# Fixed orders in a Fourier layer without GpSimd, a padded Nyquist product, and seven block products in another order

## The chip, the cores and the metric

One core of a Trainium2 chip runs the whole program. The metric is the device time of that core in microseconds for one execution, as the median of the runs. Its engines are called PE (TensorE's matmuls; PEld is its weight loads), DVE (VectorE), ACT (ScalarE), POOL (GpSimd) and SP (SyncE, which starts the DMAs here).

## What is computed

Two trunk layers over 512 tokens of 1024 channels, with a context of 256 tokens. Layer 0 has attention, layer 1 Fourier mixing; both end with a gated ConvFFN. All data is float32. Cut to the parts that the change touches:

```python
D_MODEL, SEQ, FNET_GROUPS, D_FF = 1024, 512, 4, 2816

def fourier_mix(h):                                   # layer 1
    hg = h.reshape(b, l, FNET_GROUPS, d // FNET_GROUPS).astype(F32)
    f = jnp.fft.fft2(hg, axes=(1, 3), norm="ortho").real
    return f.reshape(b, l, d).astype(h.dtype)

def conv_ffn(h, w_up, conv_w, conv_b, w_down):        # both layers
    u = h @ w_up
    up = jnp.pad(u, ((0, 0), (1, 1), (0, 0)))
    u = up[:, :-2] * conv_w[0] + up[:, 1:-1] * conv_w[1] + up[:, 2:] * conv_w[2] + conv_b
    gate, val = jnp.split(u, 2, axis=-1)
    return (jax.nn.silu(gate) * val) @ w_down
...
    h = modulate(rms_norm(x, norm_g[i, 0]), sh1, sc1)
    y = attention_mixers(...) if i % 2 == 0 else fourier_mix(h) @ w_f
    x = x + g1 * rms_norm(y, norm_g[i, 1])
    h = modulate(rms_norm(x, norm_g[i, 2]), sh2, sc2)
    x = x + g2 * rms_norm(conv_ffn(h, ffn_w_up[i], ffn_conv_w[i], ffn_conv_b[i], ffn_w_down[i]), norm_g[i, 3])
```

## The kernel before

**Numbers.** Every float32 operand of a matmul is kept as a high part (rounded to TensorE's fp32r) and a low part (the rest). `mm3` (L107) makes a product of three matmuls: high by high (L108), high by low (L109), low by high (L110), each up to 128 rows deep and some 256 columns wide. `split` (L130) makes such a pair: ScalarE casts the high part, VectorE subtracts it for the low part (L131). Weights come by DMA into one of three `raw` buffers and are split into `wh` and `wl`.

**Layout.** Channels lie on the 128 partitions in `KC = 8` chunks, the 512 tokens on the free dimension in two halves of 256 (`halves`). `xT` is the residual stream, `yT` the output of a sub-layer before its norm, `hh`/`hl` the pair of the normed input. A `misc` or `mm` tile is one PSUM bank of 512 columns.

**What sets the order.** The code is written in one order, and a scheduler then orders each engine's queue by priorities and dependencies. `follow(i, j)` puts one instruction behind another on the same engine; `fence` and `held` keep what comes after a fence behind what came ahead of it; `behind_pe` starts a generator's TensorE work behind the last matmul so far; `later(n)` lowers or raises the priority.

**Blocks of the FFN.** Layer 0 takes 10 and layer 1 takes 14 of its chunks of up-projection by a seven-product scheme: `seven_products` (L1329) makes two output tiles `x` and `y`, each one PSUM bank of two halves, from seven products "1" to "7" of 12 matmuls each. Products 1, 5, 6 and 7 are needed in two places: ScalarE copies them from PSUM to `xs` or `ys` (L1349, L1351, L1354, L1359), the next product on that bank is added on top or goes to its other half, and VectorE adds the copies to `x` and `y` (L1357, L1360). In code order the products are 1, 5, 2, 6, 4, 3, 7; only the first on a bank and those behind it are tied by `follow`. Around them run VectorE's sums of weights (L1315 to L1318), its low weights and the convolution (L1412 to L1426).

**The Fourier stage.** Between layer 0's last down products (`part(d, [1])`, second half of the tokens, d = 1 to 7) and the output panels of layer 1 the kernel ends layer 0's norm, updates `x`, and transforms. `Plain.tiles` (L410) does it for a half: the statistics' row is spread over the partitions (L234), `x_update` multiplies `yT` by the factor `der` and the row `Rs` and adds it to `xT` (L330, L332), ScalarE makes `hh` (L417), VectorE `hl` (L418), ScalarE the square (L421), and GpSimd sums six of eight chunks' squares (L423). `columns` (L478) turns those sums into a column by matmuls against ones (L483): r, the inverse norm of every token of the next input, which scales rows of the transform. `over_channels(g, h)` transforms a group's 256 channels for a half of the tokens (12 matmuls, and from them `Z`), `group(g, ts)` transforms over the token tiles `ts` of 128, six matmuls for each (cosines into A, sines into B), `tables` makes the token tables `ct` and `st`, the second half's scaled by r. `shift` transforms the constant shift. Channel 128 of each group, the Nyquist channel, has a product of its own: `cosines(None, N, ...)` gives `N`, four rows (one for each group) of 258 columns.

**Output panels.** For each of the eight panels d of 128 output channels: four products of B (12 matmuls) into `pq`, one of N (three matmuls, four rows deep, with the weights `nyh`, `nyl`) and four of A (12 matmuls) into `pp`; ScalarE copies `pq` to `qs` (L1814) and VectorE adds and subtracts the two.

## Time and profile before

| | |
|---|---|
| median of 3 runs | 1110.64 us (1109.5 to 1110.91) |
| the profiled execution | 1112.16 us |
| its span, first to last instruction | 1110.4 us |
| mean granted TensorE clock | 0.996 |
| matmuls recorded | 9220 |
| time that PE and DVE are busy | 97% and 81% of the span |

The profile is of one execution. Its page gives each engine's busy time; the trace behind it gives each instruction's start and length, and for an engine that stood idle what ended the wait, in brackets: `[1.12 <-POOL yT L423]` is 1.12 us idle, ended by GpSimd's write of `yT` on line 423. Rows of tiles read output<-inputs, then partitions x elements. Stages, by the trace: attention until about 320, layer 0's ConvFFN until about 665, the Fourier layer from there to about 729 (its output panels from 700.6), layer 1's ConvFFN until about 1085, then the end.

### The profile page before, as it was taken

The page shows a single profiled execution, that of the slowest core. Times are in us where ns is not written, and L with a number is a line of the kernel's source. Part 1 is how long each engine was busy: PE and PEld are TensorE (multiplying, and loading weights), DVE is VectorE, ACT ScalarE, POOL GpSimd, SP SyncE. Part 2 cuts the span into 40 slices and gives each one's busy share as a digit, 9 for nine tenths or more (in the row PEclk, how much of TensorE's full clock was granted, in tenths as well). Part 3 has the DMA queues.
Part 4 walks back from the last instruction along what each step waited for, and adds up shares of the span by engine and source line. Part 5 has one row for each costly group of instructions (what it writes and reads, how often), then busy time and mean ns, then how long its engine had stood idle before and what let it go on. Part 6 is the DMA issues. An engine that isn't in the chain of part 4 may idle for free.

```text
span 1110.4 us, 22277 instructions
## 1 busy us (share of the span) xinstructions
PE 1081.1 (97%) x9220; PEld 1011.4 (91%) x9220; DVE 894.8 (81%) x1459; ACT 595.2 (54%) x1048; POOL 128.5 (12%) x136
## 2 busy tenths in 40 slices
PE   9999999999999999999999998999999999999995
PEld 5699888869999999999999997989999999999995
DVE  5778877763689967878999788878997998979756
ACT  4442356665665633552556446668755654655543
POOL 0046123412100000000000133300000000000012
PEclk9999999999999999999999999999999999999998
DMA  9675100273231565227624600923205433332342
GB/s 368 273 256 209 39 7 33 76 275 143 77 153 43 181 233 213 106 86 272 236 77 175 231 22 21 279 82 143 86 29 198 145 107 118 105 103 88 106 148 77
DMA packets 33774, 156.01 MB, mean 140 GB/s; under 512 B 3460, under 2 KB 8196, under 8 KB 22024
## 3 DMA queue, kind: packets, MB, share of 16 engines
q1 hardware_dynamic: 32520, 150.39, 37.6%
q0 software_dynamic: 1152, 4.19, 1.5%
q8 instruction: 72, 1.18, 0.4%
q14 instruction: 30, 0.25, 0.1%
HBM read 148.28 MB, written 6.29 MB: 139 GB/s over the span
## 4 chain that ended last, share of the span: by engine, by line
PE 69%; DVE 18%; ACT 6%; DMA 4%; issue 2%; POOL 1%; SPq 0%; DVEq 0%; POOLq 0%; ACTq 0%
PE mm L108 20%; PE mm L109 18%; PE mm L110 18%; DVE wl L131 4%; ACT wh L131 2%; PE PT L1081 1%; DVE cv L1413 1%; DVE cv L1415 1%; DMA raw<-in_w_up 1%; DVE md_t L330 1%; DVE xT L332 1%; PE gm L108 1%; ACT yT L352 1%; PE O L109 1%; PE gm L110 1%
## 5 line engine op out<-in xcount | busy, mean ns | idle before, releaser
L131 ACT CAST wh<-raw 128x1024 fp32r<-128x1024 f32 (+2 forms) x207 | 190.7, 932 | 147.3 <-PE mm L109 96.9
L131 DVE TENSOR_TENSOR wl<-raw,wh 128x1024 fp32r<-128x1024 f32 (+2 forms) x205 | 219.4, 1076 | 59.3 <-ACT wh L131 56.7
L108 PE MATMUL mm<-hh,wh 128*128 128x256 f32 x856 | 240.2, 282 | 2.5 <-ACT sq L1351 1.8
L110 PE MATMUL mm<-hh,wl 128*128 128x256 f32 x856 | 236.9, 277 | 1.7 <-DVE wl L131 1.7
L109 PE MATMUL mm<-hl,wh 128*128 128x256 f32 x856 | 237.0, 277 | 0.4 <-DVE hl L355 0.3
L108 PEld LDWEIGHTS mm<-hh,wh 128*128 128x128 f32 x856 | 160.4, 188 | 8.5 <-ACT sq L1351 6.1
L110 PEld LDWEIGHTS mm<-hh,wl 128*128 128x128 f32 x856 | 160.9, 188 | 2.2 <-DVE wl L131 2.1
L109 PEld LDWEIGHTS mm<-hl,wh 128*128 128x128 f32 x856 | 160.8, 188 | 0.8 <-DVE hl L355 0.5
L108 PE MATMUL mm<-xh,wh 128*128 128x256 f32 x492 | 136.8, 279 | 0.0
L109 PE MATMUL mm<-xl,wh 128*128 128x256 f32 x492 | 136.6, 278 | 0.0
L110 PE MATMUL mm<-xh,wl 128*128 128x256 f32 x492 | 136.4, 277 | 0.0
L108 PE MATMUL mm<-zh,wh 128*128 128x256 f32 x384 | 109.4, 285 | 0.7 <-ACT sq L1354 0.5
L109 PE MATMUL mm<-zl,wh 128*128 128x256 f32 x384 | 106.3, 277 | 0.0
L110 PE MATMUL mm<-zh,wl 128*128 128x256 f32 x384 | 106.2, 277 | 0.0
L108 PEld LDWEIGHTS mm<-xh,wh 128*128 128x128 f32 x492 | 92.4, 188 | 1.2 <-issue 0.8
L109 PEld LDWEIGHTS mm<-xl,wh 128*128 128x128 f32 x492 | 92.4, 188 | 0.6 <-issue 0.4
L110 PEld LDWEIGHTS mm<-xh,wl 128*128 128x128 f32 x492 | 92.5, 188 | 0.1
L108 PEld LDWEIGHTS mm<-zh,wh 128*128 128x128 f32 x384 | 72.1, 188 | 6.0 <-ACT sq L1354 5.4
L110 PEld LDWEIGHTS mm<-zh,wl 128*128 128x128 f32 x384 | 72.2, 188 | 0.0
L109 PEld LDWEIGHTS mm<-zl,wh 128*128 128x128 f32 x384 | 72.1, 188 | 0.0
L305 POOL TENSOR_TENSOR gacc<-gacc,sq 128x256 f32<-128x256 f32 (+1 forms) x23 | 20.2, 880 | 396.8 <-ACT sq L303 396.4
L1412 ACT ACTIVATE cv<-mm,cols 128x512 f32<-128x512 f32 x59 | 45.8, 778 | 10.8 <-PE mm L110 6.1
(457 smaller groups left out, 2795.7 us busy)
## 6 DMA issues: line engine op xcount, KB each, us to landing
raw<-in_w_up SPq DMA_DIRECT2D x42, 1024.0 KB, 4.9
xT<-in_mod_r SPq DMA_DIRECT2D x20, 1024.0 KB, 5.0
raw<-in_w_down SPq DMA_DIRECT2D x32, 384.0 KB, 3.1
raw<-in_mod_p SPq DMA_DIRECT2D x8, 1024.0 KB, 5.0
raw<-in_w_down SPq DMA_DIRECT2D x16, 512.0 KB, 4.3
raw<-in_w_in SPq DMA_DIRECT2D x6, 1024.0 KB, 8.2
yT<-in_mod_r SPq DMA_DIRECT2D x10, 512.0 KB, 6.6
raw<-in_w_out SPq DMA_DIRECT2D x4, 1024.0 KB, 5.9
```

The source lines that it names most:

```text
L108: i = PE.matmul(out, lhsT=ah, rhs=bh, start=start, stop=False, skip_group_check=skip)
L109: PE.matmul(out, lhsT=ah, rhs=bl, start=False, stop=False, skip_group_check=skip)
L110: return i, PE.matmul(out, lhsT=al, rhs=bh, start=False, stop=stop, skip_group_check=skip)
L131: i = S.copy(out=h, in_=src), eng.tensor_tensor(out=l, in0=src, in1=f(h), op=ALU.subtract)
L305: G.tensor_tensor(out=self.acc[:, sl], in0=self.acc[:, sl], in1=sq[:, sl], op=ALU.add)
L330: m = V.scalar_tensor_tensor(out=t, in0=yT[:, k, hs], scalar=der[:, l, gi, k:k + 1], in1=R, op0=ALU.mult, op1=ALU.mult)
L332: return m, (eng or (G if k % 2 else V)).tensor_tensor(out=xT[:, k, hs], in0=xT[:, k, hs], in1=t, op=ALU.add)
L352: S.activation(out=yT[:, c, halves[h]], in_=yT[:, c, halves[h]], func=AF.Identity, bias=bm[:, c:c + 1], scale=am[:, c:c + 1])
L1081: PE.transpose(out=pt[:, j * P:(j + 1) * P], in_=Ps[j][:, off:off + P], identity=ident)
L1412: S.activation(out=cv, in_=ps, func=AF.Identity, bias=bc, scale=wc[1])
L1413: V.scalar_tensor_tensor(out=cv[:, 1:], in0=ps[:, :T - 1], scalar=wc[0], in1=cv[:, 1:], op0=ALU.mult, op1=ALU.add)
L1415: V.scalar_tensor_tensor(out=cv[:, :T - 1], in0=ps[:, 1:], scalar=wc[2], in1=cv[:, :T - 1], op0=ALU.mult, op1=ALU.add)
```

## The change

**The block products.** Code order and TensorE order become 1, 5, 6, 2, 3, 4, 7: each product's first matmul is tied behind the preceding product's last. The copies, the sums and the number of matmuls stay.

On TensorE's queue, in the first block of layer 1 before (mm_12272 and mm_12273 are its two PSUM banks; products 6, with weights `wh_12264`, and 2, with `wh_12268`; a wait for "Activation" is one for ScalarE):

```order
L110 MATMUL mm_12272<-zh_9928,wl_12261 128x256
L108 MATMUL mm_12273<-zh_9932,wh_12264 128x256 [waits Activation_49]
L109 MATMUL mm_12273<-zl_9933,wh_12264 128x256
L110 MATMUL mm_12273<-zh_9932,wl_12265 128x256 [waits DVE_49]
L108 MATMUL mm_12273<-zh_9932,wh_12264 128x256
L108 MATMUL mm_12272<-hh_69,wh_12268 128x256 [waits Activation_49]
L109 MATMUL mm_12272<-hl_71,wh_12268 128x256
L110 MATMUL mm_12272<-hh_69,wl_12269 128x256 [waits DVE_49]
L108 MATMUL mm_12272<-hh_69,wh_12268 128x256
L109 MATMUL mm_12272<-hl_71,wh_12268 128x256
```

Product 6 is begun with four matmuls, then product 2 comes in, behind ScalarE's copy of the other half of its bank; the other eight of product 6 follow product 2, and product 3 and 4 are interleaved in the same way. In the same block after (product 6 has `wh_12297`, product 2 `wh_12301`; the first row is the second matmul of product 6):

```order
L109 MATMUL mm_12306<-zl_9966,wh_12297 128x256
L110 MATMUL mm_12306<-zh_9965,wl_12298 128x256 [waits DVE_49]
L108 MATMUL mm_12306<-zh_9965,wh_12297 128x256
L109 MATMUL mm_12306<-zl_9966,wh_12297 128x256
L110 MATMUL mm_12306<-zh_9965,wl_12298 128x256
L108 MATMUL mm_12306<-zh_9965,wh_12297 128x256
L109 MATMUL mm_12306<-zl_9966,wh_12297 128x256
L110 MATMUL mm_12306<-zh_9965,wl_12298 128x256
L108 MATMUL mm_12306<-zh_9965,wh_12297 128x256
L109 MATMUL mm_12306<-zl_9966,wh_12297 128x256
L110 MATMUL mm_12306<-zh_9965,wl_12298 128x256
L108 MATMUL mm_12305<-hh_69,wh_12301 128x256 [waits Activation_49]
```

Now all twelve matmuls of product 6 stand between product 5 and product 2, and twenty-four (2 and 3) between 6 and 4.

**The Fourier stage.** GpSimd's table splits and its sums over the input's squares go; its sums over the squares of the down products (L305) stay. In place of `tiles`, `Plain` has `gated` (first half) and `spread_on` (second half) for the row, `update` and `low` for two chunks at a time, and `totals` and `columns`. The factor `der` is put on `yT` by ScalarE as each down product ends (after L1470), the update is a multiplication and an addition 512 columns wide, the squares stay in `yT`, and TensorE sums them: `totals` is 64 small matmuls with ones for a half, `rstd` as everywhere else, and `columns` two small matmuls that turn the row into a column. The DFT table splits go from GpSimd to VectorE. `in_turn` ties the TensorE instructions of each step behind those of the one before, and the same for VectorE, so that both engines run the list of steps as it is written. The first half's sums stand behind down product 6 and its column behind 7; `shift` comes late, by the second half's column.

On TensorE before, around the second half's column (misc_8288; L483; `wh_7989` is a token table and `hh_69` the normed input):

```order
L108 MATMUL mm_8193<-wh_7989,Z_1032_7992 128x256
L109 MATMUL mm_8193<-wl_7990,Z_1032_7992 128x256
L110 MATMUL mm_8193<-wh_7989,Z_1033_7993 128x256
L483 MATMUL misc_8288<-ones_7_70,yT_68 128x2 [waits DVE_49,Pool_49]
L483 MATMUL misc_8288<-ones_7_70,yT_68 128x2 [waits Activation_49]
L483 MATMUL misc_8288<-ones_7_70,yT_68 128x2 x2
L108 MATMUL misc_8314<-wh_7987,hh_69 128x256 [waits DVE_49]
L109 MATMUL misc_8314<-wl_7988,hh_69 128x256
L110 MATMUL misc_8314<-wh_7987,hl_71 128x256
```

The column's four matmuls stand behind the token products of group 2 and wait for GpSimd's sums. After, at the same place (L211 is the sum by ones, of `totals`):

```order
L110 MATMUL mm_8247<-wh_8026,Z_1033_8030 128x256
L211 MATMUL misc_8267<-yT_68,ones_7_70 32x64 [waits DVE_49]
L211 MATMUL misc_8267<-yT_68,ones_7_70 32x64 x7
L211 MATMUL misc_8267<-yT_68,ones_7_70 32x64 [waits Activation_49]
L211 MATMUL misc_8267<-yT_68,ones_7_70 32x64 x7
L211 MATMUL misc_8267<-yT_68,ones_7_70 32x64 [waits Activation_49]
L211 MATMUL misc_8267<-yT_68,ones_7_70 32x64 x7
L211 MATMUL misc_8267<-yT_68,ones_7_70 32x64 [waits Activation_49]
L211 MATMUL misc_8267<-yT_68,ones_7_70 32x64 x7
L108 MATMUL misc_8308<-wh_8024,hh_69 128x256 [waits DVE_49]
L109 MATMUL misc_8308<-wl_8025,hh_69 128x256
L110 MATMUL misc_8308<-wh_8024,hl_71 128x256 [waits DVE_49]
```

The sums over the squares are now on TensorE, behind group 3; the column itself comes 24 matmuls later, after `shift`.

**The Nyquist product.** `N`, `nyh` and `nyl` have 128 rows instead of 4, the rest zeros: `w_ny` is padded on the host side of the layout (512 KB instead of 16 KB), its pair is made behind the fence, and N's tiles are set to zero on VectorE ahead. The Nyquist cosines become the last of the token products, behind group 3.

On ScalarE ahead of the first panel before (N_1024 is N's high part; qs the copy of the panel's B product):

```order
L131 CAST N_1024_7978<-mm_8384 4x258 [waits DVE_49]
L131 CAST B_1020_7974<-mm_8193 128x512 [waits PE_49]
L131 CAST A_1022_7976<-mm_8301 128x258 [waits DVE_49]
L131 CAST wh_8559<-yT_68 128x1024 [waits DVE_49,Activation_49]
L1814 COPY qs_8450<-mm_8421 128x256 [waits PE_49]
```

and after:

```order
L144 CAST B_1020_8011<-mm_8247 128x512 [waits PE_49]
L144 CAST A_1022_8013<-mm_8195 128x258 [waits DVE_49]
L144 CAST A_1022_8013<-mm_8240 128x258 [waits DVE_49]
L144 CAST A_1022_8013<-mm_8254 128x258 [waits DVE_49]
L1888 COPY qs_8483<-mm_8454 128x256 [waits PE_49]
L144 CAST N_1024_8015<-mm_8434 4x258 [waits DVE_49]
```

The cast of N now stands behind the copy of the first panel's B product, which waits for TensorE.

The diff, cut to its core (`in_turn` and the class first, then the calls in their new order):

```diff
+    def in_turn(step, *args):
+        ops = nc.cur_bb.bb.instructions
+        at = len(ops)
+        r = step(*args)
+        for o in [o for o in ops[at:] if o.engine in turn]:
+            if turn[o.engine] is not None:
+                tc.add_manual_dep(o, turn[o.engine], mybir.DependencyInfo(
+                    mybir.DependencyClass.NoSync, mybir.DependencyReason.DATA), reason="order")
+            turn[o.engine] = o.name
+        return r
...
+        def gated(self, ys, pps, am):
+            r = rstd(ys.sums(pps, 0)[:, :W4])
             yield
+            self.h, self.am = 0, am
+            self.R = [spread(r, pps)] * 2
+            yield
+            for k in range(0, KC, 2):
+                self.update(k)
+                self.low(k)
+
+        def spread_on(self, r, pps):
+            Rp, _ = spread(r, pps, copy=False)
+            R = mk(cp, [P, HT], F32, "Rs", 3)
+            S.copy(out=R, in_=Rp)
+            self.h, self.R = 1, (Rp, R)
+
+        def update(self, k):
+            x, y = (v[:, k:k + 2, halves[self.h]] for v in (xT, yT))
+            t = md(True)
+            V.tensor_tensor(out=t, in0=y, in1=both(self.R[k > 0]), op=ALU.mult)
+            V.tensor_tensor(out=x, in0=x, in1=t, op=ALU.add)
+            if k == KC - 2:
+                S.activation(out=y, in_=x, func=AF.Square)
+            for c in (k, k + 1):
+                S.activation(out=hst[:, c, halves[self.h]], in_=xT[:, c, halves[self.h]], func=AF.Copy,
+                             scale=self.am[:, c:c + 1])
+            if k < KC - 2:
+                S.activation(out=y, in_=x, func=AF.Square)
+
+        def low(self, k):
+            hs = halves[self.h]
+            for c in (k, k + 1):
+                V.scalar_tensor_tensor(out=lst[:, c, hs], in0=xT[:, c, hs], scalar=self.am[:, c:c + 1],
+                                       in1=f(hst[:, c, hs]), op0=ALU.mult, op1=ALU.subtract)
+
+        def totals(self, h, pps):
+            ps = mk(pps, [P, T], F32, "misc", 2)
             for k in range(KC):
-                x_update(h, l, gi, R, k, eng)
-                x = xT[:, k, hs]
-                S.activation(out=hst[:, k, hs], in_=x, func=AF.Copy, scale=am[:, k:k + 1])
-                V.scalar_tensor_tensor(out=lst[:, k, hs], in0=x, scalar=am[:, k:k + 1], in1=f(hst[:, k, hs]),
-                                       op0=ALU.mult, op1=ALU.subtract)
-                sq = mk(cp, [P, T], F32, "sq", 2)[:, :HT] if 0 < k < KC - 1 else (self.last if k else self.acc)[:, hs]
-                S.activation(out=sq, in_=x, func=AF.Square)
-                if 0 < k < KC - 1:
-                    G.tensor_tensor(out=self.acc[:, hs], in0=self.acc[:, hs], in1=sq, op=ALU.add)
-                if k % 2:
-                    yield
-
+                stat_add(ps, yT[:, k, halves[h]], HT, k == 0, k == KC - 1)
+            return ps
...
-        def columns(self, h, pps):
-            ps = mk(pps, [P, T], F32, "misc", 2)
-            for i in range(2):
-                t = 2 * h + i
-                for n, s in enumerate((self.acc, self.last)):
-                    PE.matmul(ps[:, 2 * i:2 * i + 2], lhsT=s[:, t * P:(t + 1) * P], rhs=ones32[:, :2], start=n == 0,
-                              stop=n == 1)
-            return rstd(ps[:, :4])
+        def columns(self, h, r, ps):
+            for b in range(2):
+                PE.matmul(ps[64 * b:64 * b + 64, :2], lhsT=r, rhs=con[:, K_QD + b:K_QD + 4:2], start=True, stop=True)
+            if not h:
+                self.rc = mk(fx, [P, 4, 2, 3], F32, "ub")[:, 0, :, :2]
+            with later(-10000):
+                V.tensor_copy(out=self.rc[:, h], in_=ps[:, :2])
...
-            if new:
-                begun[id(ps)] = m[-1]
-            else:
-                follow(m[0], begun[id(ps)])
+            begun[id(ps)] = True
+            if last:
+                follow(m[0], last.pop())
+            last.append(m[-1])
 
         product("1", y, 1)
         S.copy(out=xs[:, :HT], in_=y[:, HT:])
         product("5", x, 1)
         S.copy(out=ys[:, HT:], in_=x[:, HT:])
-        product("2", x, 0)
         product("6", y, 1)
         S.copy(out=xs[:, HT:], in_=y[:, HT:])
-        product("4", y, 0)
+        product("2", x, 0)
         product("3", x, 1)
         V.tensor_tensor(out=x, in0=x, in1=xs, op=ALU.add)
+        product("4", y, 0)
         product("7", y, 1)
         S.copy(out=ys[:, :HT], in_=y[:, HT:])
         V.tensor_tensor(out=y, in0=y, in1=ys, op=ALU.add)
...
+                if l == 0:
+                    S.activation(out=yT[:, d, sl], in_=yT[:, d, sl], func=AF.Copy, scale=der[:, 0, 3, d:d + 1])
...
+    def first_norms():
+        with later(-10000):
+            r = rstd(plain.totals(0, pps)[:, :W4])
+        yield
+        plain.columns(0, r, mk(pps, [P, T], F32, "misc", 2))
+
+    norms = first_norms()
...
-        N = [mk(up, [4, 320], F32R, "N%d" % i)[:, :M1] for i in range(2)]
+        N = [mk(up, [P, 320], F32R, "N%d" % i)[:, :M1] for i in range(2)]
...
-        split(ft[0], ft[1], raw([P, 2, 256], a["dft_c"]), G)
+        split(ft[0], ft[1], raw([P, 2, 256], a["dft_c"]))
...
+        fences.clear()
+        table(st, ls, 0)
+        sb = [mk(fx, [P, KC], F32R, "sh%d" % i) for i in range(2)]
+        split(sb[0], sb[1], n1[1])
+        nyh, nyl = wpair([P, D])
+        for v in N:
+            V.memset(f(v), 0.0)
+
+        in_turn(over_channels, 0, 0)
+        scaled(0)
+        in_turn(rest_of, 0)
+        v1 = in_turn(rstd, in_turn(ys.sums, pps, 1)[:, :W4])
+        in_turn(over_channels, 1, 0)
+        in_turn(over_channels, 2, 0)
+        in_turn(plain.spread_on, v1, pps)
+        in_turn(over_channels, 3, 0)
+        in_turn(table, ct, lc, 0)
+        scaled(1)
+        in_turn(rest_of, 1)
+        in_turn(plain.update, 0)
+        scaled(2)
+        in_turn(rest_of, 2, [0])
+        in_turn(plain.low, 0)
...
+        in_turn(group, 2, [0, 1])
+        in_turn(group, 3, [0, 1])
+        ps = in_turn(plain.totals, 1, pps)
+        r = in_turn(rstd, ps[:, :W4])
+        in_turn(over_channels, 2, 1)
+        in_turn(plain.low, 6)
+        in_turn(plainly, 2)
+        in_turn(shift, sb, ps[:, 128:])
+        in_turn(plain.columns, 1, r, ps[:, 192:])
+        in_turn(over_channels, 3, 1)
+        in_turn(table, ct, lc, 2)
+        in_turn(table, st, ls, 2)
+        in_turn(plainly, 3)
+        in_turn(table, ct, lc, 3)
+        in_turn(table, st, ls, 3)
+        fb = in_turn(shifted, ps[:, 128:])
...
+        ny = raw([P, D], a["w_ny"])
+        held(S.copy(out=nyh, in_=ny))
+        held(V.tensor_tensor(out=nyl, in0=ny, in1=f(nyh), op=ALU.subtract))
+        for g in range(4):
+            in_turn(group, g, [2])
+        for g in range(4):
+            in_turn(group, g, [3])
+        in_turn(cosines, None, [v[:4] for v in N], [z[:, :, :, P] for z in Z], list(range(TT)), True)
...
-               w_out=w_out, w_up=w_up, w_f=w_f, w_ny=wf[:, P])
+               w_out=w_out, w_up=w_up, w_f=w_f, w_ny=np.concatenate([wf[:, P], np.zeros((P - 4, D), wf.dtype)]))
```

More of the change, by code (lines that the diff above doesn't have):

```diff
@@ L1332, in seven_products @@
         xs, ys = (mk(cp, [P, T], F32, "sq", 2) for _ in range(2))
-        begun = {}
+        begun, last = {}, []
         def product(n, ps, h):
@@ L1707, in shift, with scaled @@
-        def shift():
-            b = [mk(fx, [P, KC], F32R, "sh%d" % i) for i in range(2)]
-            split(b[0], b[1], n1[1])
-            ps = mk(pps, [P, T], F32, "misc", 2)
+                    mm3(ps[:, i, :], hst[:, k, ts_], lst[:, k, ts_], ft[0][:, c, :], ft[1][:, c, :],
+                        i + c == 0, i + c == 2)
+            Zp[g] = ps
+        def scaled(g):
+            for t in range(2):
+                S.activation(out=Z[0][:, t, g, :], in_=Zp[g][:, t, :], func=AF.Copy, scale=plain.rc[:, 0, t:t + 1])
@@ new lines @@
+        in_turn(group, 0, [0, 1])
+        in_turn(over_channels, 0, 1)
+        in_turn(rest_of, 2, [1])
+        in_turn(plain.update, 2)
+        scaled(3)
+        in_turn(rest_of, 3, [0])
+        in_turn(plain.low, 2)
+        in_turn(group, 1, [0, 1])
+        in_turn(over_channels, 1, 1)
+        in_turn(rest_of, 3, [1])
+        in_turn(plainly, 0)
+        in_turn(plain.update, 4)
+        in_turn(plain.update, 6)
+        in_turn(plainly, 1)
+        in_turn(plain.low, 4)
+        in_turn(group, 2, [0, 1])
@@ L1793 @@
-        cosines(None, N, [z[:, :, :, P] for z in Z], list(range(TT)), fb[:4, 4:5])
-        group(3, [2, 3])
         zs.close()
```

91 lines of the change are left out of this document (29 added, 62 removed).

## The prediction

> **What bounds the kernel now.** I read the page's busy shares first, then a window over the Fourier stage, then the waits, then the rows in the two places that the change touches.
>
> The page's top (busy microseconds, share of the span, instructions):
>
> ```profile
> span 1110.4 us, 22277 instructions
> PE 1081.1 (97%) x9220; PEld 1011.4 (91%) x9220; DVE 894.8 (81%) x1459; ACT 595.2 (54%) x1048; POOL 128.5 (12%) x136
> ```
>
> TensorE sets the time: 97% busy, with VectorE next at 81%. So only three things can shorten it: TensorE's idle time, stretches in which its matmuls follow each other more slowly than they could, and matmuls themselves. The windows show the first two for the Fourier stage (length, then busy time of PE, PEld, DVE, ACT and POOL with counts, the granted clock, DMA share and GB/s), from the last down product of layer 0 to the first matmul of the output panels:
>
> ```profile
> 662.50:700.60 38.10, 34.13 (x292) 32.10 (x291) 32.48 (x82) 22.60 (x56) 11.09 (x13) 0.96 0.16 48
> 691.20:694.60 3.40, 3.40 (x18) 3.40 (x18) 2.35 (x7) 2.31 (x5) 0.00 (x0) 0.50 0.00 0
> ```
>
> TensorE idles for 38.10 - 34.13 = 3.97 us of the stage, and 3.40 us run at half the clock. The larger of its stalls, with their releasers (in brackets: idle time, and what ended it):
>
> ```profile
> 668.42 0.54 PE L198 MATMUL misc<-cv,ones 128*32 128x64 f32 x24 [0.56 <-POOL cv L305]
> ...
> 673.79 0.45 PE L234 MATMUL misc<-Rs,con 128*128 128x256 f32 x1 [1.06 <-DVE Rs L229]
> ...
> 683.18 0.28 PE L110 MATMUL misc<-wh,hl 128*128 128x256 f32 x1
> 684.14 0.39 PE L110 MATMUL misc<-wh,hl 128*128 128x256 f32 x1 [0.68 <-DVE hl L418]
> 684.36 0.28 PE L108 MATMUL misc<-wh,hh 128*128 128x256 f32 x1
> ...
> 686.41 0.39 PE L108 MATMUL misc<-wh,hh 128*128 128x256 f32 x1 [0.23 <-DVE Z L131]
> ...
> 689.57 0.38 PE L483 MATMUL misc<-ones,yT 128*128 128x2 f32 x2 [1.12 <-POOL yT L423]
> ```
>
> A stall costs more than its idle time: from 683.18 to 684.36 two steps take 1.18 us instead of 0.24, that is 0.94 for 0.68 idle. Five stalls at 0.26 more add 1.3. Half clock costs half of 3.40, 1.7. Together 3.97 + 1.3 + 1.7 = **7.0 us lost** in this stage, and 31.1 us of work. GpSimd and VectorE end these waits.
>
> The block steps, once in each of the 24 blocks (start, length, engine):
>
> ```profile
> 1000.71 0.28 PE L108 MATMUL mm<-zh,wh 128*128 128x256 f32 x1
> 1001.33 0.39 PE L108 MATMUL mm<-hh,wh 128*128 128x256 f32 x1 [0.35 <-ACT sq L1351]
> 1001.55 0.28 PE L109 MATMUL mm<-hl,wh 128*128 128x256 f32 x1
> ...
> 1001.89 0.62 ACT L131 CAST xh<-cv 128x512 fp32r<-128x512 f32 x1 [0.61 <-DVE cv L1426]
> ...
> 1003.61 0.28 PE L110 MATMUL mm<-zh,wl 128*128 128x256 f32 x1
> ...
> 1003.92 0.37 ACT L1354 COPY sq<-mm 128x256 f32<-128x256 f32 x1 [1.41 <-PE mm L110]
> ...
> 1004.06 0.28 PE L108 MATMUL mm<-hh,wh 128*128 128x256 f32 x1
> ...
> 1004.35 0.38 PE L108 MATMUL mm<-zh,wh 128*128 128x256 f32 x1
> ```
>
> Between 1001.55 and 1003.61 lie eighteen steps: 0.114 us each. The step into 1001.33 takes 0.62 and the next 0.22: 0.61 us lost. The step into 1004.35 takes 0.29. Each time TensorE stands before a product whose PSUM bank ScalarE is still copying out. The group of the waits by weight loads (total, times, longest) has them all:
>
> ```profile
> PEld mm L108 <- ACT sq L1351: 6.1, 20, 0.6
> PEld mm L108 <- ACT sq L1354: 5.4, 24, 0.7
> ```
>
> That is 11.5 us in 44 waits. The first stall above lost 0.61 for the longest value there, 0.6; the slow second step, 0.22 for 0.114, comes behind each wait. I take 0.07 more per wait, between nothing and that 0.11: 11.5 + 44 x 0.07 = **14.6 us** (11.5 to 16.3).
>
> **The change part by part.** *Block steps.* From the start of product 6's last matmul (1003.61) to the copy's end (1003.92 + 0.37 = 1004.29) and TensorE's restart (1004.35) pass 0.74 us. Before, four matmuls of another product cover it (0.46). After, twelve do (12 x 0.114 = 1.37 us) for the copies of 1 and 5 and twenty-four for that of 6, so the handoff is hidden with 0.6 to spare; only a cast of 0.62 us or more that ScalarE has just begun uses that up. I leave 0.7 us for such meetings over all blocks. What is late next is VectorE, which makes the low weights:
>
> ```profile
> 336.00:360.00 24.00, 24.00 (x214) 23.97 (x212) 24.00 (x31) 13.58 (x20) 0.00 (x0) 1.00 0.13 45
> 580.00:605.00 25.00, 24.83 (x213) 24.24 (x212) 24.76 (x34) 13.76 (x22) 0.00 (x0) 1.00 0.38 130
> 880.00:910.00 30.00, 28.59 (x241) 27.61 (x240) 28.70 (x38) 16.89 (x26) 0.00 (x0) 1.00 0.35 121
> ```
>
> In these 79 us VectorE is 24.00 of 24, 24.76 of 25 and 28.70 of 30 us busy: there a shorter TensorE waits for weights instead. Of the some 559 us of block stages (336 to 640 and 815 to 1070) they are 14%, 2.1 us of the 14.6; with stretches just below that I take 2.5. The third loss is the matmuls' own spacing:
>
> ```profile
> 656.77 0.28 PE L108 MATMUL mm<-xh,zh 128*128 128x256 f32 x1
> ...
> 657.85 0.28 PE L108 MATMUL mm<-xh,zh 128*128 128x256 f32 x1
> ```
>
> Nine steps in 1.08 us are 0.120 each, against the 0.114 above. Where stalls vanish such slow stretches may last longer: with a twentieth of the blocks' some 4,900 matmuls (559 us by 0.114), 245 more at 0.006 us are 1.5, an estimate between nothing and the rival below. Sum: -14.6 + 0.7 + 2.5 + 1.5 = **-9.9, say -10**.
>
> *Fourier stage.* The rows of what goes and of what comes, the new two-chunk forms from their twins in the second layer's update, and TensorE's sums by ones (48 in one piece of the chain of waits):
>
> ```profile
> L332 DVE TENSOR_TENSOR xT<-xT,md_t 128x256 f32<-128x256 f32 x16 | 9.6, 618 | 0.0
> L418 DVE SCALAR_TENSOR_TENSOR hl<-xT,der,hh 128x256 fp32r<-128x256 f32 x16 | 9.5, 595 | 0.0
> L423 POOL TENSOR_TENSOR yT<-yT,sq 128x256 f32<-128x256 f32 x12 | 11.4, 946 | 17.6 <-ACT sq L421 17.2
> L483 PE MATMUL misc<-ones,yT 128*128 128x2 f32 x16 | 2.0, 249 | 1.1 <-POOL yT L423 1.1
> ...
> L449 DVE TENSOR_TENSOR xT<-xT,md_t 128x512 f32<-128x512 f32 x7 | 4.6, 687 | 0.1
> L452 DVE SCALAR_TENSOR_TENSOR hl<-xT,der,hh 128x256 fp32r<-128x256 f32 x16 | 7.1, 481 | 1.4 <-ACT hh L451 1.4
> ...
> 752.05 0.81 PE mm L198 x48
> ```
>
> GpSimd's twelve additions of L423 go (11.4 us, the last of them releaser of the 1.12 us wait). VectorE's two update operations, 16 x 618 ns each, become 8 x 687 each, and the lower halves 16 x 481 instead of 595: 9.6 + 9.6 + 9.5 = 28.7 becomes 5.5 + 5.5 + 7.7 = 18.7 us. Against these 10 us stand the tables' splits, now VectorE's: three of some 512 columns, 2.1 us by the 687. So VectorE has 8 us less, 24.5 instead of 32.48. Whether 481 or 595 applies is bounded by 1.8 us on an engine with that slack. The factor put on ScalarE is 16 more of its operations, 6 to 10 us by the rows of its copy (0.37) and its cast (0.62), beside 22.60 busy of 38.10: covered; without that cover it would end up on the path of the down products.
>
> The Trainium skill ("GPSIMD Engine Reference", section 1, on its specifications) says that GpSimd shares its SBUF ports with VectorE; by that rule the 595 and 618 next to GpSimd's work against 481 and 687 for twice the columns are contention, and the trace agrees.
>
> TensorE gets the sums: 64 small matmuls per half, 64/48 x 0.81 = 1.08, with a slow entry 1.25 each, 2.5 in all; four column products in two pairs, each some 0.4 by the first row of L483 above (0.38); and loses the sixteen of L483, some 1.75 (busy 2.0, overlapping). That is +1.5: work 32.6. The waits that stay I put at 1.5 (the statistics of the down products, whose last GpSimd sum, 0.56 above, now has `shift` no longer ahead of it; and the chain from TensorE's sums over VectorE's row to `columns(1)`), between nothing and all 7.0. So the stage takes 34.1 instead of 38.1: **-4.0** (+1.5 to -5.5).
>
> *The Nyquist product.* One output panel, its last B matmul, the three of N, the first of A, and the ScalarE cast that makes N before the first panel:
>
> ```profile
> 699.72 0.36 ACT L131 CAST N<-mm 4x258 fp32r<-4x258 f32 x1
> ...
> 709.27 0.28 PE L110 MATMUL mm<-B,wl 128*128 128x256 f32 x1
> 709.48 0.38 PE L108 MATMUL mm<-N,wh 4*128 4x258 f32 x1
> 709.70 0.28 PE L109 MATMUL mm<-N,wh 4*128 4x258 f32 x1
> ...
> 710.03 0.39 PE L108 MATMUL mm<-A,wh 128*128 128x258 f32 x1
> 710.26 0.28 PE L109 MATMUL mm<-A,wh 128*128 128x258 f32 x1
> ```
>
> From 709.27 to 710.26 are five steps in 0.99 us, against 0.60 at 0.120 each: 0.39 lost at going into the four-row form and out of it. With 128 rows N has the form of A and B; eight panels give 8 x 0.39 = **-3.1**. I take that whole, since both entries show it (709.48 and 710.03) and the A matmuls are the very form that N gets; the other end is no gain. The weights' 512 KB instead of 16 KB are asked for before the panels' own and split behind the tables, one cast and one subtraction on engines with slack. Against it stands the order on ScalarE: the first panel's copy (0.37 by the twin above) now comes before the N cast (0.36), and TensorE waits for both behind its B product. Before, it waited for the cast alone; I add 0.6, between 0 and 0.37 + 0.36 + 0.31 (the distance from a last matmul to its copy, above) = 1.0.
>
> The Trainium skill ("TensorEngine Tiling (Array Packing)", Key Properties) says that changing the tiling mode drains TensorE; the steps into 709.48 and 710.03 agree. Another page of it speaks against the change and is rival D.
>
> Sum: -10 - 4.0 - 3.1 + 0.6 = **-16.5**, from the profiled execution's span of 1110.4 to 1093.9. What lies around the span doesn't change; that execution lasted 1112.16, the median of the runs shown is 1110.64, 0.14% less. Off the median the forecast is **1094.1**.
>
> **The rivals.** *A, slower: the slow spacing takes over.* Place: the block stages, some 4,900 matmuls. If waits are what ends a slow stretch, and 38 of 44 go, every one may run at 0.120: 4,900 x 0.006 = 29 us. That turns -16.5 (with its 1.5 taken out, -18) into +11: 1122. It decides from 18/0.006 = 3,000 slow matmuls on. For it: both spacings stand in the rows, and no row names what chooses between them. Against: long stretches between two waits run at 0.114 too, as the eighteen steps do. 5%.
>
> *B, VectorE and the weights take over in the blocks.* With two steps of 0.28 to 0.61 saved per block, the low weights become the last to come in most blocks, not in 14%. For it: 24.00 of 24 above. Against: VectorE's 81% over the span. Of the 10 us some 1 is left: 1103. 15%.
>
> *C, the fixed orders stall.* PE and DVE take turns by a list; one late item holds all behind it, and the sums of the second half wait for ScalarE's squares. The 4.0 goes: 1098. For it: the chain of statistics, update, square, sum and column is as long as before, and the half clock may come back behind its pauses. Against: 8 us less on VectorE. 17%.
>
> *D, padding is worth nothing.* The Trainium skill ("TensorE: Matmul & The Clock Gate", "Why this matters for your kernels") says that a single matmul with few rows (K=32) takes as long as one with K=128; by that rule N has nothing to gain. The rows agree on length (0.28 for the second N matmul, as for A) and differ on the entries. If the 0.39 belongs to the order of operands rather than to the form, the -3.1 goes: 1097. 8%.
>
> *E, the handoff only moves.* Product 6 now waits for the copy of 1 behind twelve matmuls; casts like the 0.62 one meet it in every block: 24 x 0.28 = 6.7 back, 1101. Against: 0.6 to spare. 7%.
>
> *F, the change doesn't do what it says:* the scheduler could undo the order. Its rows show it doing it; 1%.
>
> **How the numbers follow.** My forecast 47%, A 5%, B 15%, C 17%, D 8%, E 7%, F 1%. The likeliest alone: 1094.1, with its bounds put together (blocks from -6.8 to -13.5 by the 11.5 and the 16.3 with and without the terms behind them, Fourier stage from -2.5, with twice the waits, to -5.5, N from -2.1 to -3.1) 1088.5 to 1099. Rivals C, D and E lie within 1097 to 1101, B at 1103 with its own spread, so the range is 1088 to 1104.5; outside stay A and the upper side of B with others beside it. Faster by over 0.2% (2.2 us, about what a measurement of this kernel can tell from no change) is every case but A, F and B together with C: 0.90. Within 0.2%: 0.04. Slower: A and a share of the unforeseen, 0.06.
>
> **What would show it.** In the profile after: waits of weight loads for ScalarE's copies in the blocks down from 11.5 us to under 2, with VectorE's low weights grown in their place by some 2.5; steps into N and out of it of 0.12 in all eight panels; one wait of some 1 us at the first N; the window from the last down product to the first panel 34 us long with VectorE some 24.5 busy and no stall ended by L423's additions. Wrong would make it: product 6 waiting for the copy of 1, matmuls of the blocks at 0.120 on the whole, or a half clock in the Fourier stage.

## The result and the profile after

The kernel after takes 1097.28 us (median of 4 runs, 1095.7 to 1098.07) against 1110.07 us (1109.07 to 1110.91): a ratio of 0.9872, 95% interval 0.9853 to 0.9892, so 12.0 to 16.3 us faster. In a second comparison it came to 0.9856 (0.9835 to 0.9878). The forecast was 1094.1 us, 16.5 less, in a range of 1088.0 to 1104.5.

The profiled execution of the kernel after lasted 1097.22 us. The top of its page:

```profile
span 1095.4 us, 22485 instructions
PE 1068.3 (98%) x9340; PEld 1008.1 (92%) x9340; DVE 891.7 (81%) x1450; ACT 600.4 (55%) x1055; POOL 113.0 (10%) x121
```

TensorE is busy 12.8 us less, with 120 matmuls more. The windows of the Fourier stage (from the last down product to the first panel), of the output panels, and of layer 1's blocks, with the columns as before:

```profile
660.00:692.30 32.30, 31.80 (x354) 30.08 (x347) 23.75 (x61) 18.66 (x42) 0.00 (x0) 1.00 0.12 42
692.30:721.90 29.60, 27.01 (x218) 25.87 (x216) 25.26 (x39) 22.10 (x43) 12.87 (x13) 1.00 0.98 285
825.00:1040.70 215.70, 214.91 (x1875) 213.97 (x1874) 193.06 (x251) 123.61 (x197) 0.00 (x0) 1.00 0.38 126
```

The Fourier stage lost its stalls (0.50 us idle instead of 3.97), its half clock (1.00 instead of 0.96) and GpSimd; VectorE is 23.75 us busy in it instead of 32.48. The panels are the opposite: TensorE idles for 2.6 of 29.60 us there. In the kernel before, the same windows of panels and blocks read:

```profile
700.60:729.40 28.80, 28.80 (x218) 26.46 (x216) 22.11 (x33) 20.98 (x40) 13.08 (x13) 1.00 1.00 302
832.70:1055.60 222.90, 220.45 (x1874) 214.34 (x1874) 190.47 (x249) 123.60 (x196) 0.00 (x0) 1.00 0.36 121
```

Before, TensorE never idled in the panels. The blocks' waits by weight loads for ScalarE's copies, 6.1 and 5.4 us before, read after:

```profile
PEld mm L108 <- ACT sq L1381: 1.2, 2, 0.7
PEld mm L108 <- ACT sq L1379: 0.9, 3, 0.3
```

And this is how a handoff looks in the timeline of the kernel after, the one that took 0.62 us before:

```profile
988.41 0.37 ACT L1381 COPY sq<-mm 128x256 f32<-128x256 f32 x1
...
989.29 0.28 PE L109 MATMUL mm<-zl,wh 128*128 128x256 f32 x1
989.40 0.28 PE L110 MATMUL mm<-zh,wl 128*128 128x256 f32 x1
989.51 0.28 PE L108 MATMUL mm<-hh,wh 128*128 128x256 f32 x1
```

The copy ends at 988.78; the product that needs its bank begins at 989.51 in the steady step, with 0.73 us to spare.

Where the time went, by the same marks in the trace of every kernel (the copies of product 1 and the last copy of a layer's blocks, the first matmul of the last down product, of the panels, the last of the panels, the last matmul); lengths in us, each from one profiled execution:

| stage | before | after | after, 2nd | blocks only | rest only | padding only | N last, timed |
|---|---|---|---|---|---|---|---|
| start to layer 0's first block copy | 358.9 | 357.5 | 357.0 | 360.8 | 356.9 | 358.6 | 359.1 |
| to layer 0's last block copy | 248.5 | 244.6 | 244.4 | 244.9 | 249.0 | 248.5 | 244.9 |
| to the last down product | 55.1 | 58.0 | 56.5 | 55.3 | 56.4 | 55.2 | 57.9 |
| to the first panel | 38.1 | 32.3 | 32.2 | 39.0 | 32.3 | 37.6 | 32.3 |
| panels | 28.8 | 29.5 | 29.7 | 28.8 | 29.8 | 25.7 | 28.3 |
| to layer 1's first block copy | 103.2 | 103.2 | 104.0 | 104.0 | 103.2 | 105.8 | 102.8 |
| to layer 1's last block copy | 222.9 | 215.6 | 217.6 | 215.6 | 222.2 | 223.4 | 215.4 |
| to the last matmul | 43.9 | 43.9 | 43.8 | 43.9 | 43.9 | 43.8 | 43.9 |

The first row is code that no kernel changes. It scatters by 3.9 us between these executions, so a difference of 2 us between two profiles means nothing unless its stage and its rows say so.

### The profile page after: what moved, and what is told of

It is laid out like the page before. It is cut to its first block, busy times and chain, and to the rows that moved or that the text cites. A ratio compares the mean times of both kernels' runs of the same rounds, so it can differ in the third digit from the quotient of the medians.

```text
span 1095.4 us, 22485 instructions
## 1 busy us (share of the span) xinstructions
PE 1068.3 (98%) x9340; PEld 1008.1 (92%) x9340; DVE 891.7 (81%) x1450; ACT 600.4 (55%) x1055; POOL 113.0 (10%) x121
## 4 chain that ended last, share of the span: by engine, by line
PE 75%; DVE 13%; ACT 5%; DMA 4%; issue 2%; POOL 0%; DVEq 0%; POOLq 0%; SPq 0%; ACTq 0%
PE mm L108 20%; PE mm L110 20%; PE mm L109 20%; DVE wl L144 3%; PE PT L1112 1%; ACT wh L144 1%; PE gm L108 1%; DVE gacc L566 1%; DVE cv L1443 1%; DVE cv L1445 1%; PE gm L109 1%; PE gm L110 1%; ACT yT L365 1%; PE O L109 1%; PE S L108 1%
## 5 line engine op out<-in xcount | busy, mean ns | idle before, releaser
L144 ACT CAST wh<-raw 128x1024 fp32r<-128x1024 f32 (+2 forms) x206 | 190.0, 931 | 150.0 <-PE mm L109 103.2
L108 PE MATMUL mm<-zh,wh 128*128 128x256 f32 x384 | 107.1, 279 | 0.3
```

The costliest lines, as they stand in the source:

```text
L108: i = PE.matmul(out, lhsT=ah, rhs=bh, start=start, stop=False, skip_group_check=skip)
L144: i = S.copy(out=h, in_=src), eng.tensor_tensor(out=l, in0=src, in1=f(h), op=ALU.subtract)
```

## The experiments

**The block order alone.** Edit: `seven_products` as after, all else as before.

```diff
-        product("2", x, 0)
         product("6", y, 1)
         S.copy(out=xs[:, HT:], in_=y[:, HT:])
-        product("4", y, 0)
+        product("2", x, 0)
         product("3", x, 1)
```

> The kernel before with the block products in the new order and nothing else. If the block part stands by itself: 9 to 10 us faster than before (the two profiled executions give 3.0 in layer 0's blocks and 6.7 in layer 1's), some 1100.5, with the waits of weight loads for the copies out of PSUM at 2 us or less instead of 11.5. Rival: the blocks gain only because the Fourier stage leaves earlier and the weights have more lead; then under 6 us.

Measured: ratio 0.9911 (0.9894 to 0.9928), 9.9 us faster than the 1112.15 beside it. Its waits of weight loads:

```profile
PEld mm L108 <- ACT sq L1350: 1.2, 2, 0.7
PEld mm L108 <- ACT sq L1348: 0.9, 2, 0.7
```

2.1 us instead of 11.5, and the blocks take 3.6 and 7.3 us less by the table. The interval of the gain, 8.0 to 11.8 us, lies above the rival's 6: the part stands by itself.

**All but the block order.** Edit: the kernel after with the old `seven_products`.

```diff
+        product("2", x, 0)
         product("6", y, 1)
         S.copy(out=xs[:, HT:], in_=y[:, HT:])
-        product("2", x, 0)
+        product("4", y, 0)
         product("3", x, 1)
```

> The kernel after with the block products in the old order. By the two profiled executions 4.6 us come off the stage up to the first output panel and 0.7 us are given back in the panels: 3.9 us faster than before, some 1106. By my prediction's terms, if the panels' waits come from the blocks' part of the change: 6.5 us faster. Rival: the gain of the Fourier stage lies in its fixed orders only together with the new block order: no change.

Measured: 0.9948 (0.9932 to 0.9963), 5.8 us (4.1 to 7.6). Stage by stage it is the kernel after up to the panels (32.3) and in them (29.8): 3.5 us together, with 1.3 in the row ahead for the first half's sums. The 2.0 us in the first row are the scatter named above. The interval leaves out the 3.9 us that the two profiles gave and holds the 6.5 of the prediction's terms, but the reason given for 6.5 is not borne out: the panels wait here as in the kernel after. With the blocks' 9.9 that is 15.7, inside both intervals of the whole: nothing that can be measured is gained or lost between the two parts.

**The padding alone.** Edit in the kernel before:

```diff
-        N = [mk(up, [4, 320], F32R, "N%d" % i)[:, :M1] for i in range(2)]
+        N = [mk(up, [P, 320], F32R, "N%d" % i)[:, :M1] for i in range(2)]
...
-        nyh, nyl = wpair([4, D])
-        split(nyh, nyl, raw([4, D], a["w_ny"]))
+        for v in N:
+            V.memset(f(v), 0.0)
+        nyh, nyl = wpair([P, D])
+        split(nyh, nyl, raw([P, D], a["w_ny"]))
```

> The kernel before with N, its weights and their load padded to 128 rows and nothing else. If the steps into and out of the four-row form cost 0.39 us in each of eight panels, as its profile shows: 3.1 us faster, 1107, and steps of 0.12 there. If the panels' weights are due so closely that they take it back: 0 to 1.5 us faster, with waits for the low weights in the panels. If the steps belong to the order of operands: no change, and steps of 0.2 stay.

Measured: 0.9977 (0.9961 to 0.9992), 0.9 to 4.3 us. The trace is plainer. Its panels:

```profile
699.80:725.50 25.70, 25.70 (x218) 25.48 (x216) 21.17 (x31) 18.80 (x36) 12.13 (x13) 1.00 0.99 302
```

25.7 us for 28.8: the 3.1 that the eight entries and exits promised, with TensorE busy throughout. So it is the four-row form that costs 0.39 us a panel, not the order of operands, and in the kernel after these 3.1 us are spent on something else. Even here this execution gave back 2.6 us right behind the panels (105.8 for 103.2 in the table). Some 1.7 of it is the matmuls' spacing, which is as slow there with the blocks only; TensorE also idles 0.8 us more, with a wait for GpSimd's last sum of squares that the kernel before doesn't have:

```profile
PE misc L198 <- POOL acc L305: 1.0, 1, 1.0
```

**The kernel after, again.**

> The changed kernel a second time, for what differs between executions. If the 2.4 us gained ahead of layer 0's FFN (code that is the same in both kernels) and the places where matmuls run at 0.118 are chance, this execution has them elsewhere and its span differs by up to 2 us from 1095.4; if they belong to the kernel, the head again ends 2.4 us earlier than before's and the slow stretches lie at the same places (317 to 370, 542 to 575, 811 to 885).

Measured: 1098.32 us (1093.55 to 1098.62), profile span 1096.3. The head again took about 357 us, and 356.9 with "rest only". But "N last, timed", which has the kernel after's code there too, needs 359.1, and "four rows again" below 359.8: most of it is chance, not the change. The panels' length came back to 0.2 us, the Fourier stage's to 0.1. The slow stretches did not stay: layer 1's blocks took 217.6 us instead of 215.6, and a window in them at full TensorE time holds 343 matmuls in place of 357, in the first and in the second execution:

```profile
890.00:930.00 40.00, 40.00 (x357) 39.46 (x356) 38.36 (x51) 23.93 (x38) 0.00 (x0) 1.00 0.33 109
```

```profile
890.00:930.00 40.00, 40.00 (x343) 39.46 (x343) 37.85 (x50) 22.34 (x37) 0.00 (x0) 1.00 0.34 113
```

Same code, same clock, no idle time: 0.112 against 0.117 us for a matmul.

**What holds the panels: GpSimd's sums left out.** The timeline of the kernel after at two of the panels' stalls (POOL is GpSimd):

```profile
695.22 0.39 PE L108 MATMUL mm<-N,wh 128*128 128x258 f32 x1 [0.72 <-ACT N L144]
...
714.16 2.24 DVE L1800 TENSOR_TENSOR gacc<-raw 128x512 f32<-128x512 f32 x1
714.25 1.58 POOL L318 TENSOR_TENSOR acc<-acc,sq 128x512 f32<-128x512 f32 x1
...
717.51 1.23 DVE L144 TENSOR_TENSOR wl<-gacc,wh 128x1024 fp32r<-128x1024 f32 x1 [0.78 <-ACT wh L144]
...
718.79 0.38 PE L110 MATMUL mm<-B,wl 128*128 128x256 f32 x1 [0.76 <-DVE wl L144]
```

A VectorE sum of 0.67 us takes 2.24 beside a GpSimd addition; the cast behind it starts late, then the low weights, then the matmul. The experiment takes the additions away; its output lacks those sums.

```diff
+            if self.direct > 1 and n < KC - self.direct:
+                return
             if n < KC - self.direct:
                 G.tensor_tensor(out=self.acc[:, sl], in0=self.acc[:, sl], in1=sq[:, sl], op=ALU.add)
```

> The kernel after, leaving out five additions of squares on GpSimd in the output panels (so the norm behind them lacks those sums). Theory: the panels' low weights are late because VectorE is slowed by GpSimd beside it (additions of 0.67 us that take 1.46 to 2.24); then without GpSimd's additions these rows take 0.7, the waits for low weights in panels 3 to 6 (some 2.3 us) go, and the panels take 27.3 instead of 29.6 us. Rival: they are late since the work on them starts only when the Fourier stage's last splits are done; then the rows get shorter and more than half of the wait stays.

Measured, in one execution: the panels take 27.30 us (the two of the kernel after differ by 0.2 there). The two groups of these sums, of the kernel after and then without the additions (line numbers moved by two):

```profile
L1800 DVE TENSOR_TENSOR gacc<-raw 128x512 f32<-128x512 f32 x4 | 4.3, 1067 | 0.0
...
L1799 DVE TENSOR_TENSOR gacc<-raw 128x512 f32<-128x512 f32 x4 | 3.5, 868 | 0.0
```

```profile
L1802 DVE TENSOR_TENSOR gacc<-raw 128x512 f32<-128x512 f32 x4 | 2.7, 678 | 0.0
L1801 DVE TENSOR_TENSOR gacc<-raw 128x512 f32<-128x512 f32 x4 | 2.7, 676 | 0.0
```

The four sums of each line go from 1067 and 868 ns to 678 and 676, the waits for low weights are gone, and these are TensorE's waits that stay in the panels:

```profile
PE mm L108 <- ACT N L144: 0.7, 1, 0.7
PE mm L109 <- DVE B L144: 0.4, 1, 0.4
```

The theory holds for the waits, and the rival falls: no wait for low weights stays. The page "GPSIMD Engine Reference" of the Trainium skill (section 1) says that the two engines share SBUF ports; these rows agree, with 2.24 us in place of 0.67 for the longest of them.

The stretching alone is not enough, though. With the padding alone, VectorE's sums are stretched as far, and TensorE never idles in the panels:

```profile
717.61 2.24 DVE L1758 TENSOR_TENSOR gacc<-raw 128x512 f32<-128x512 f32 x1
```

What differs is the lead. The first of these sums behind the Fourier stage's own work, in the kernel before and after, whose panels begin at 700.60 and 692.32:

```profile
696.93 0.68 DVE L1757 TENSOR_TENSOR gacc<-raw 128x512 f32<-128x512 f32 x1
```

```profile
695.54 0.67 DVE L1799 TENSOR_TENSOR gacc<-raw 128x512 f32<-128x512 f32 x1
```

3.7 us ahead of the panels became 3.2 us behind their beginning. The second fence, which holds these sums back, stands ahead of the last token products in the kernel before and behind the Nyquist cosines in the kernel after. So the waits come where VectorE is stretched and starts late; without the one (this run) or the other (the padding alone) they are not there. That a start as early as before would end them in the kernel after was not tried.

**N behind A.** Edit in the kernel after:

```diff
-            mm3(pp[:, :M1], nyh[:, d * P:(d + 1) * P], nyl[:, d * P:(d + 1) * P], N[0], N[1], True, False)
             for g in range(4):
-                mm3(pp[:, :M1], wh[:, 0, g, :], wl[:, 0, g, :], A[0][:, g, :], A[1][:, g, :], False, g == 3)
+                mm3(pp[:, :M1], wh[:, 0, g, :], wl[:, 0, g, :], A[0][:, g, :], A[1][:, g, :], g == 0, False)
+            mm3(pp[:, :M1], nyh[:, d * P:(d + 1) * P], nyl[:, d * P:(d + 1) * P], N[0], N[1], False, True)
```

> The kernel after with the product of N behind those of A in each panel instead of ahead of them. The wait for the cast of N (a step of 0.99 us) is then hidden: panels 0.9 us shorter, 28.7. Rival: the wait goes over to the A products, whose pairs come at the same time: 29.4 or more.

Measured: panels of 28.3 us to the end of N's three matmuls, which now close them: 1.2 less than 29.5, a little more than expected. N's wait is gone, and so is the one for B's low part, since the scheduler also puts A matmuls ahead of the B matmul that waited for it. (The 27.9 us that later expectations name end ahead of the last panel's N.) What is left there is the low weights:

```profile
PE mm L110 <- DVE wl L144: 1.6, 3, 0.6
```

**Without the second fence.** Edit: the `fence()` behind the Nyquist cosines goes, in the kernel after, and in the one with N last.

```diff
         in_turn(cosines, None, [v[:4] for v in N], [z[:, :, :, P] for z in Z], list(range(TT)), True)
-        fence()
         zs.close()
```

> The kernel after without the second fence, the one behind the Nyquist cosines, so that VectorE may make the panels' weights in the gaps of the last splits of A, B and N. If the late start of the weights is what holds the panels: the low weights of panels 2 to 6 come 2 us or more earlier, the waits for them go, and the panels take 27 to 27.5 us instead of 29.6; some 1095. If GpSimd's slowing of VectorE decides: 29 us or more. A cost is possible at the first panel: B's low part may come up to 1.2 us later behind a split of weights.

> Both: N last and no second fence. If the two effects add, the panels take 26.3 us and the kernel is 3.2 us faster than the one after: a ratio of 0.9840 to the kernel before where the one after has 0.9872. If one fence's gain is lost at the first panel, 0.986.

Measured: 0.9935 (0.9914 to 0.9957) and 0.9917 (0.9894 to 0.9939). Against the first ratio of the kernel after (0.9872) this is slower by 7 and 5 us; the panels take 36.7 and 33.5 us. Both expectations failed. The first of the two, on TensorE and on ScalarE:

```profile
703.44 0.58 PE L108 MATMUL mm<-N,wh 128*128 128x258 f32 x1 [7.29 <-ACT N L144]
...
702.07 1.06 ACT L1312 ACTIVATE xl<-xh 128x1024 fp32r<-128x1024 f32 x1 [5.52 <-DMA xh<-in_w_up]
703.04 0.35 ACT L144 CAST N<-mm 4x258 fp32r<-4x258 f32 x1
```

With the fence gone, a ScalarE operation on layer 1's weights, fed by a GpSimd DMA, is queued ahead of N's cast. It waits 5.52 us for that DMA, N's cast behind it, and TensorE 7.29 us behind both, and then runs at half clock for a while (the mean over the panels is 0.86). I had looked at VectorE's queue for what the fence holds back; it was ScalarE's that mattered.

**Four rows again in the kernel after.** Edit: the padding undone.

> The kernel after with N, its weights and their load at four rows again. If the padding is worth 3.1 us wherever it stands: the panels take 32.7 instead of 29.6 us. If the panels wait for their low weights, a slower TensorE only waits less: 30.3 to 31.3 us, the steps into and out of N at 0.2 and the waits for low weights down from 2.3 to under 1 us.

Measured: panels of 32.0 us. No wait for low weights is left in them. But the clock is not the same:

```profile
692.40:724.40 32.00, 30.89 (x218) 28.12 (x216) 23.08 (x39) 22.46 (x43) 12.74 (x13) 0.95 0.92 269
```

0.95 of 32.00 us is 1.6 us lost to half clock, which neither execution of the kernel after shows in the panels (1.00). Without it 30.4 would stand, an estimate, within the second expectation: where the low weights are late, most of the padding's 3.1 us turn into waiting. Whether the four-row form brought the half clock on, one execution doesn't tell.

**Sums of the weights ahead of the fence.** Edit, with N last: only VectorE's two sums are freed, the casts stay behind the fence.

```diff
-            held(V.tensor_tensor(out=pm[:, 0, :, :], in0=r[:, :, 0, :], in1=r[:, :, 1, :], op=ALU.add))
-            held(V.tensor_tensor(out=pm[:, 1, :, :], in0=r[:, :, 1, :], in1=r[:, :, 0, :], op=ALU.subtract))
+            V.tensor_tensor(out=pm[:, 0, :, :], in0=r[:, :, 0, :], in1=r[:, :, 1, :], op=ALU.add)
+            V.tensor_tensor(out=pm[:, 1, :, :], in0=r[:, :, 1, :], in1=r[:, :, 0, :], op=ALU.subtract)
```

> N last in each panel (27.9 us in the panels when it was tried alone), and VectorE's two sums that begin a panel's weights no longer held behind the fence; the casts on ScalarE stay behind it. If it was the casts and the work of ScalarE in front of N's cast that cost 7 us without the fence, and the late start of the weights costs the rest: no wait of over 1 us at N, the low weights 1 us or more earlier, the panels at 27 us. Rival: B's and A's low parts come later by the sums (0.67 us each) and the panels take 28.5 or more.

Measured: panels of 30.0 us, the rival's side. N no longer waits, the low weights wait more than with N last alone:

```profile
PE mm L110 <- DVE wl L144: 2.7, 3, 1.5
```

The low weights of the first two panels made here come 1.6 and 2.5 us earlier than with N last alone, counted from the first panel, the next ones no earlier: the wait went over to the later panels. Freeing these two sums is not enough; a start of all the weights ahead of the panels stays untried.

**The squares added on VectorE.** Edit, with N last:

```diff
-                G.tensor_tensor(out=self.acc[:, sl], in0=self.acc[:, sl], in1=sq[:, sl], op=ALU.add)
+                (V if self.direct > 1 else G).tensor_tensor(out=self.acc[:, sl], in0=self.acc[:, sl], in1=sq[:, sl],
+                                                            op=ALU.add)
```

> N last in each panel, and the additions of squares in the panels on VectorE instead of GpSimd. GpSimd beside it stretched VectorE's rows by some 4.3 us in all; the five additions cost it 5 x 0.68 = 3.4. If the stretching is what counts: waits for low weights (2.4 us with N last) down to 1.5, the panels at 27 us. If VectorE's load alone counts: 27.5 to 28.5, no gain.

Measured: panels of 28.8 us, which hold sixteen of the norm's small matmuls that otherwise stand behind them; no gain over 28.3. The waits for low weights are 1.0 us instead of 1.6. What GpSimd's additions cost VectorE is about what they cost it on its own queue.

**N behind A, timed.**

> The kernel after with N last in each panel, now timed: the best of the versions tried by the panels' length (27.94 us against 29.5 and 29.7). If that length holds, the panels take 27.9 again and the kernel is 1.7 us (0.15%) faster than the one after: a ratio of 0.984 to 0.986 to the kernel before. If it was chance of one execution, the panels take 29.5 and the ratio is 0.986 to 0.987.

Measured: 1095.21 us (1093.61 to 1097.21), 0.9864 (0.9839 to 0.9889). The panels' window again:

```profile
694.10:722.40 28.30, 26.76 (x218) 25.96 (x216) 22.46 (x39) 21.85 (x43) 12.68 (x13) 1.00 0.96 289
```

28.3 us a second time, so the panels are 1.2 to 1.4 us shorter than in the two executions of the kernel after. The intervals of the whole overlap with those of the kernel after (0.9872 and 0.9856): the time of the whole doesn't tell them apart.

## Why the prediction was right, and where it was off

- **Block waits (-14.6, part back).** Right in mechanism and place: 11.5 us of waits became 2.1, as "under 2" said but for 0.1, and in the handoff shown the copy is done 0.73 us early where 0.6 was worked out. Rival E is out. The blocks by the table took 11.2 us less (3.9 and 7.3) where -10 was forecast, and 9.4 less in the second execution. The bound of -13.5 doesn't come out of the terms named for it (16.3 less 4.7 is 11.6, without them 16.3).
- **VectorE as next bound (2.5 back).** Oversized. TensorE's waits for low weights over the whole span, before and after:

```profile
PE mm L110 <- DVE wl L131: 1.7, 2, 1.0
```

```profile
PE mm L110 <- DVE wl L144: 2.1, 4, 0.8
```

  They grew by 0.4, and 1.1 of the 2.1 lie in the panels. Counted by weight loads, as the forecast was, the blocks' waits for low weights are 1.2 us before, 1.3 and 0.8 in the two executions after. A VectorE that is busy 24.00 of 24 us was not one that TensorE waited for. Rival B is out for the blocks.
- **The spacing (1.5 back).** The slow spacing of rival A exists, at a tenth to a fifth of its price. In layer 1's blocks the steps between 0.1155 and 0.127 us went from 120 to 504, and to 978 in the second execution; by what they take beyond 0.1133 this is 0.6, 2.3 and 4.4 us. In layer 0's blocks it is 1.3, 2.1 and 2.8. So 2.5 us more than in the one execution of the kernel before stood there in one and 5.3 in the other. That the missing stalls bring this is not shown: over all fourteen executions, the slow steps cost 0.05 to 4.4 us in layer 1's blocks and 0.6 to 3.7 in layer 0's with the new order, against 0.6 to 0.9 and 1.3 to 2.6 in the three with the old one.
- **Fourier stage (-4.0).** Right: 5.8 us shorter, less the first half's sums of some 1.3 that now lie ahead of the mark: -4.5. No half clock, and waits of 0.50 where 1.5 was put. VectorE has 23.75 us of work where 24.5 was worked out, but that is partly luck: the prediction took all 48 rows of the update for both halves (28.7 us), of which this window held 30 before (16.3), and 2.1 us left it because three sums of the panels' weights moved behind it, into the panels.
- **Padding (-3.1) and N's cast (+0.6).** The padding's price was exact in the panels, as its own experiment shows. In the kernel after, N's steps run through, here the panel's last B, N's three and the first A:

```profile
698.42 0.28 PE L110 MATMUL mm<-B,wl 128*128 128x256 f32 x1
698.54 0.28 PE L108 MATMUL mm<-N,wh 128*128 128x258 f32 x1
698.66 0.28 PE L109 MATMUL mm<-N,wh 128*128 128x258 f32 x1
698.78 0.28 PE L110 MATMUL mm<-N,wl 128*128 128x258 f32 x1
698.90 0.28 PE L108 MATMUL mm<-A,wh 128*128 128x258 f32 x1
```

  Rival D is out. The rule of the Trainium skill ("TensorE: Matmul & The Clock Gate", "Why this matters for your kernels"), as I had turned it against the change, goes with it: a four-row matmul does take the same 0.28 us, and it is the change of form that costs. The wait for N's cast came as foreseen (a step of 0.99 and one of 0.22, some 1.0 lost, the upper bound instead of the 0.6).
- **The step that failed: "I take that whole".** The padding was priced in panels where TensorE waited for nothing. The kernel after brings TensorE to the panels some 8 us earlier, and the panels' weights, made by VectorE beside GpSimd's additions, don't come earlier by as much (their first sum by 1.4 us, 695.54 for 696.93). They became the bound: -2.5 was forecast for the panels, +0.7 to +0.9 measured. The parts add up to the +0.7: -3.1 for the padding, +1.0 for N's cast, +0.6 for the wait for B's low part in the first panel (0.38 us idle and the slow steps around it), which the prediction doesn't have, and the 2.2 that leaving out GpSimd's additions took away, which it puts at nothing. I asked what hides an edit's cost, and not what a faster stage ahead takes from the cover of the next.

Sum by the first execution: blocks -11.2, Fourier stage with the sums -4.5, panels +0.7: -15.0 (1.5 less in the head and a wait of 1.4 ahead of the last down product, which the second execution doesn't have, cancel). The forecast of -16.5 lies 0.2 us outside the first interval of the whole (12.0 to 16.3). The miss of 3.2 us in the panels is partly made up by 1.2 us more from the blocks and 0.5 from the Fourier stage; that the whole was not further off owes something to luck, as the blocks' 9.4 in the second execution shows.

## What to carry to other kernels

Give a copy out of PSUM as many matmuls of other banks as its whole way takes (here 0.74 us from the last matmul, so seven, and twelve cover it), and count the weight loads' waits to see what that is worth. When a stage is shortened, ask of the next stage which of its inputs are made in the meantime: a saving priced where nothing waits is spent where something does. A fence that seems to hold back only useful work also holds back what would stand in front of it; look at every engine's queue before taking it out, and at what starts later when it is moved.

## What was not expected of the hardware

**A matmul spacing that holds from one disturbance to the next.** I counted, over the traces of all fourteen profiled executions, the stretches of twelve or more matmuls that follow each other in 0.10 to 0.127 us, in layer 0 from 300 us to 660 and in layer 1 from 760 to 1085. Of 576, by the median of their first and of their last twelve steps, 416 began and ended fast (below 0.1163 us, most at 0.113) and 157 slow (most at 0.118); 3 changed on the way, each in the last down products ahead of the Fourier stage. All other changes lie at a step outside these bounds, so at a stall, a change of form or a matmul missing from the trace. The same stall at the same place can go either way; this is the kernel after, and then the first execution of N last, at the same wait for low weights:

```profile
811.84 0.39 PE L110 MATMUL mm<-hh,wl 128*128 128x256 f32 x1 [0.63 <-DVE wl L144]
812.06 0.28 PE L108 MATMUL mm<-hh,wh 128*128 128x256 f32 x1
```

```profile
812.93 0.39 PE L110 MATMUL mm<-hh,wl 128*128 128x256 f32 x1 [0.63 <-DVE wl L144]
813.16 0.28 PE L108 MATMUL mm<-hh,wh 128*128 128x256 f32 x1
```

In the trace's nanoseconds (the rows are rounded) the step between the two is 226 in the first and 221 in the second; behind the first, TensorE ran at 0.118 until 884, behind the second at 0.113 until 868. Where stalls are few, one spacing holds for long: between the two executions of the kernel after it made 2.0 us in layer 1's blocks alone. What decides between the two stays open.

**VectorE beside GpSimd.** Additions of 128x512 on GpSimd stretched VectorE's sums of the same size from 0.68 us to 2.24, and taking five of them away took 2.2 us off a stage in which TensorE never waited for GpSimd itself.
